# A fp32 network's third mixer with the value projection between two heads' scores, and its fourth mixer with the state space part in chunks of 8 steps

## The chip, the cores and the metric

The kernel runs on one core of one Trainium2 chip. The metric is the device time of one execution in microseconds (us); the number given for a kernel is the median of its runs. The engines have short names: PE (TensorE, matmuls), DVE (VectorE), ACT (ScalarE), POOL (GpSimd), SP (SyncE, which issues most of the DMAs).

## The reference, cut to what matters

The network has 512 positions and 1024 channels, in fp32. Two first layers (retention and stick breaking; gated recurrence) are followed by a second block: a third mixer, a SwiGLU feed-forward, a fourth mixer and another feed-forward, each inside `x + rmsnorm(fn(rmsnorm(x)))`. The change touches the third and the fourth mixer.

```
def even_mixer_2(t, ...):                       # third mixer
    proj = t @ w_in                             # q, k, v of 512 columns each, conv value and gate
    y_a = diff_attention(proj[..., :1536])      # 4 heads x 2 softmaxes of 64 dims, values of 128
    #   p = softmax(masked q k / 8);  w = p[:,:,0] - lam * p[:,:,1];  o = rmsnorm(w @ v, subln) * (1 - lam_init)
    y_b = conformer_conv(proj[..., 1536:])      # u = a * sigmoid(g); causal 31-tap depthwise conv; layernorm; silu
    return concatenate([y_a, y_b]) @ w_out

def odd_mixer_2(t, ...):                        # fourth mixer
    proj = t @ w_in                             # u of 256 columns, latents of 256 and 128, key rotation of 64
    y_c = s5_ssm(proj[..., :256])
    y_d = mla_attention(...)                    # 6 heads, 128 + 64 rotated dims, values of 128
    return concatenate([y_c, y_d]) @ w_out

def s5_ssm(u, ...):                             # 16 groups of 16 channels, 64 complex states each
    ab = exp(lr * dt) * (cos(li * dt) + i sin(li * dt))
    x[t] = ab * x[t-1] + bb @ u[t]              # complex, by associative_scan over 512 steps
    y = Re(c @ x) + d_skip * u
    z = gelu(y)
    return z * sigmoid(z @ w_glu + b_glu)
```

Both softmaxes are masked in chunks of 64 positions. The fp32 products of the projections are made of three passes each over operands split into a high and a low part.

## The kernel before, in words

The class `Net` writes one Python function per stage; a tile framework then sets the order of each engine's instructions once, by priorities (the order of the code, shifted by `self.prio(offset)`), by data and by free buffers. `hold(r, after)` adds a dependence by hand. An engine runs its instructions in that order.

Weights come in pieces of up to 512 KB: `wload` (L122) issues the DMA on SP into `wr` (3 buffers), ACT casts the high part `wh` (L133), DVE subtracts to get the low part `wl` (L116). `mm3` (L143) issues three matmuls (L145, L148, L149) for each product; `projT` (L155) gives outputs with channels on partitions, `projS` (L168) with positions on partitions. Activations lie in tiles `A4` (128 x 2048, 14 of them) and `U` (128 x 512, 13); PSUM has banks P (2), Z (3), W (2) and O (1). `outp` (L276) is an output projection with residual and norms; four of its weight pieces go into large buffers `wb`.

**Third mixer, `even2` (L722).** The convolution's gate is a sigmoid (L777). Three of its four channel blocks are made by 31 taps on DVE (L790), at a low rank; the fourth goes through `shifted` (L743, shifted copies by way of DRAM) and `conv_pe` (L758, matmuls L764). `scores(h)` (L815) computes a head's two softmaxes in four row blocks: matmuls L822, row maximum and exponential in `softmax_rows` (L413), difference L831, then transposes (`evac_wt`, tiles `pw` to `wt`). `av_` (L839) calls `head` (L372): value products L368, squares and a copy on ACT (L378, L379), a sum on DVE (L380). `stats` (L842), `norm` (L858) and `silu` (L863) finish the convolution's half, `heads` (L873) the attention's, in which `over_rms` scales by the root mean square. L884 to L897 set the sequence.

**Fourth mixer, `odd2` (L1017).** `s5_setup` (L924) runs during the feed-forward before it. It makes, for each of 8 pairs of groups (j), tables of cosine and sine over 512 steps and the input matrices, and stores them in DRAM (`rot`). In the mixer `s5(j, t)` (L1063) loads one table (`tab`), computes the input maps (`bur`, `bui`, L1070), rotates them (L1074 to L1076), makes two scans over 512 steps (L1077) and rotates back (L1078 to L1083); `s5_out` (L1088) multiplies by the output matrices into `py`. `s5_step` (L1101) places the eight: three ahead of the heads, one after each of the first five. `attn(hd)` (L1166) is a head's softmax, `av2` (L1182) its value product, issued in the next head. After the heads come gelu (L1208), the gated product and the sigmoid (L1220).

```
        for hd in range(6):
            attn(hd)
            s5_step(1, "P")
            if hd >= 2:
                self.lo(*late.pop(0))
```

## Time and profile before

| what | us |
|---|---|
| median of 3 runs | 1715.67 |
| lowest, highest run | 1712.09, 1715.69 |
| the profiled execution's own time | 1711.21 |
| its span, first to last instruction | 1709.4 |
| PE busy | 1656.5 |
| DVE busy | 950.2 |
| ACT busy | 677.7 |

The mean granted clock of TensorE is 0.987 of 2.4 GHz. A busy PE is not PE at its peak: matmuls are pipelined and their ends are modelled, so records overlap. "Idle before" names the engine or DMA that ended a wait. A window's line gives start and end from the span's start, its length, then busy us and instruction count of each engine, the granted clock and the DMA engines' share.

### The profile page before, as it was taken

Reading aid. Unit: us, or ns where it says so; the run is one execution under the profiler, and the core shown is the slowest. Engines: PE = TensorE matmul, PEld = TensorE weight load, DVE = VectorE, ACT = ScalarE, POOL = GpSimd, SP = SyncE. Lnnn points to the kernel's source line nnn. Section 1 sums busy time; section 2 is a strip of 40 time slices with the busy share of each in tenths; the row PEclk is TensorE's granted clock in tenths of the full one; section 3 lists DMA queues with packets and bytes.
Section 4 is the critical chain, followed back from the end, with each engine's and each line's share of the span. In section 5 each row is a group of like instructions: output and inputs, shape, how many; then the busy total and the mean of one; then the engine's idle time right before and its main releaser. Section 6 shows DMA issues by size and latency. Waiting matters only on the chain.

```text
span 1709.4 us, 20684 instructions
## 1 busy us (share of the span) xinstructions
PE 1656.5 (97%) x8072; PEld 1323.6 (77%) x8072; DVE 950.2 (56%) x1801; ACT 677.7 (40%) x1192; POOL 2.0 (0%) x8
## 2 busy tenths in 40 slices
PE   8999999999999999799999999999889999999998
PEld 8657788987789775588888878886447988888886
DVE  7564456765667994663222288468695622224332
ACT  6453334214545254643222254334556522223231
POOL 0000000000000000000000000000000000000000
PEclk9999999999999998899999999999999999999999
DMA  5212252202153220252222246432005332222341
GB/s 203 85 38 74 91 181 105 75 25 99 62 205 116 74 87 33 84 187 99 99 99 97 91 151 200 165 123 81 31 31 197 111 100 99 99 95 90 99 160 50
DMA packets 53169, 179.07 MB, mean 105 GB/s; under 512 B 5696, under 2 KB 8256, under 8 KB 52944
## 3 DMA queue, kind: packets, MB, share of 16 engines
q1 hardware_dynamic: 43824, 146.20, 25.6%
q10 hardware_dynamic: 9216, 31.48, 4.9%
q8 instruction: 63, 1.03, 0.2%
q14 instruction: 34, 0.28, 0.1%
q0 software_dynamic: 32, 0.07, 0.0%
HBM read 159.63 MB, written 18.10 MB: 104 GB/s over the span
## 4 chain that ended last, share of the span: by engine, by line
PE 85%; DVE 7%; ACT 4%; DMA 2%; issue 1%; ACTq 0%; DVEq 0%; SPq 0%
PE pp L145 17%; PE pp L148 17%; PE pp L149 17%; PE y L145 7%; PE y L149 7%; PE y L148 7%; PE pt L203 2%; PE po L368 2%; PE pl L625 1%; PE pw L203 1%; PE sc L822 1%; PE po L481 1%; DMA wr<-in_e2out 1%; PE pc L764 0%; DMA nw<-in_nw 0%
## 5 line engine op out<-in xcount | busy, mean ns | idle before, releaser
L116 DVE TENSOR_TENSOR wl<-wr,wh 128x1024 fp32r<-128x1024 f32 (+2 forms) x224 | 271.3, 1213 | 343.8 <-ACT wh L133 338.5
L133 ACT CAST wh<-wr 128x1024 fp32r<-128x1024 f32 (+2 forms) x224 | 233.4, 1043 | 523.4 <-PE pp L148 399.2
L148 PE MATMUL pp<-xl,wh 128*128 128x512 f32 (+1 forms) x1184 | 428.5, 362 | 0.0
L145 PE MATMUL pp<-xh,wh 128*128 128x512 f32 (+1 forms) x1184 | 426.0, 361 | 1.2 <-ACT xh L235 1.2
L149 PE MATMUL pp<-xh,wl 128*128 128x512 f32 (+1 forms) x1184 | 425.8, 360 | 0.0
L145 PEld LDWEIGHTS pp<-xh,wh 128*128 128x128 f32 x1184 | 223.8, 190 | 35.6 <-ACT xh L235 2.5
L148 PEld LDWEIGHTS pp<-xl,wh 128*128 128x128 f32 x1184 | 224.7, 190 | 33.8 <-issue 1.9
L149 PEld LDWEIGHTS pp<-xh,wl 128*128 128x128 f32 x1184 | 224.4, 190 | 33.4 <-issue 2.1
L145 PE MATMUL pp<-wh,xh 128*128 128x512 f32 (+1 forms) x320 | 126.4, 395 | 1.4 <-ACT sg L777 1.4
L148 PE MATMUL pp<-wl,xh 128*128 128x512 f32 (+1 forms) x320 | 126.5, 395 | 0.0
L149 PE MATMUL pp<-wh,xl 128*128 128x512 f32 (+1 forms) x320 | 125.4, 392 | 0.0
L145 PE MATMUL y<-wh,ah 128*128 128x512 f32 x288 | 112.7, 391 | 0.2
L148 PE MATMUL y<-wl,ah 128*128 128x512 f32 x288 | 112.3, 390 | 0.0
L149 PE MATMUL y<-wh,al 128*128 128x512 f32 x288 | 112.2, 389 | 0.0
L1238 DVE TENSOR_TENSOR act<-g,pp 128x512 f32<-128x512 f32 x44 | 30.2, 686 | 132.8 <-PE pp L149 131.4
L145 PEld LDWEIGHTS pp<-wh,xh 128*128 128x128 f32 x320 | 60.2, 188 | 13.4 <-ACT sg L777 1.8
L148 PEld LDWEIGHTS pp<-wl,xh 128*128 128x128 f32 x320 | 60.3, 188 | 11.7 <-issue 1.1
L149 PEld LDWEIGHTS pp<-wh,xl 128*128 128x128 f32 x320 | 60.2, 188 | 11.5 <-issue 0.6
L145 PEld LDWEIGHTS y<-wh,ah 128*128 128x128 f32 x288 | 54.1, 188 | 12.4 <-ACT bbz L998 1.1
L322 DVE TENSOR_TENSOR yn<-y,nw 128x512 f32<-128x512 f32 x48 | 31.8, 686 | 56.9 <-ACT yn L320 52.7
L790 DVE SCALAR_TENSOR_TENSOR ycv<-up,vec,ycv 128x512 f32<-128x512 f32 x90 | 63.2, 739 | 0.4
L149 PEld LDWEIGHTS y<-wh,al 128*128 128x128 f32 x288 | 54.1, 188 | 11.1
(381 smaller groups left out, 2335.0 us busy)
## 6 DMA issues: line engine op xcount, KB each, us to landing
wr<-in_f0gu SPq DMA_DIRECT2D x44, 512.0 KB, 3.3
wr<-in_f1gu SPq DMA_DIRECT2D x44, 512.0 KB, 3.3
wr<-in_f0d SPq DMA_DIRECT2D x22, 512.0 KB, 3.6
wr<-in_f1d SPq DMA_DIRECT2D x22, 512.0 KB, 3.4
xd<-x ACTq DMA_DIRECT2D x20, 512.0 KB, 2.7
x<-xd ACTq DMA_DIRECT2D x20, 512.0 KB, 6.1
wr<-in_o1t SPq DMA_DIRECT2D x16, 512.0 KB, 3.6
nw<-in_nw ACTq DMA_DIRECT2D x12, 512.0 KB, 7.8
```

What stands on the lines that cost most here:

```text
L116: return self.nc.vector.tensor_tensor(l, src, h.bitcast(F32), ALU.subtract)
L133: c = nc.scalar.copy(h, raw)
L145: r = mm(out, lhsT=a[0], rhs=b[0], start=first, stop=False)
L148: mm(out, lhsT=a[0], rhs=b[1], start=False, stop=False)
L149: return mm(out, lhsT=a[1], rhs=b[0], start=False, stop=last)
L203: self.nc.tensor.transpose(out, in_, self.ident)
L322: nc.vector.tensor_tensor(yn[j], yb[b][j], postw[j], ALU.mult)
L368: self.nc.tensor.matmul(po[:, tb * P : tb * P + P], lhsT=wt[:, sb, tb * P : tb * P + P], rhs=v[:, sb, c], start=sb == 0, stop=sb == tb)
L481: nc.tensor.matmul(po[r, sb * P :], lhsT=sv[:, sb, h * 64 : h * 64 + 64], rhs=wt[:, sb, sb * P :], start=sb == 0, stop=sb == 3)
L625: nc.tensor.matmul(pl[:, c4 * 64 : c4 * 64 + 64].rearrange("p (n x) -> p n x", x=H), lhsT=k[:, c4 * P : c4 * P + P], rhs=rh, start=True, s ...
L790: V.scalar_tensor_tensor(y, up[:, j : j + 512], self.v("dw", 4 * j + t), y, ALU.mult, ALU.add)
L1238: nc.vector.tensor_tensor(act[k // 4][:, k % 4], g, ps, ALU.mult)
```

## The change

**Third mixer.** The convolution's last two weight pieces are projected before the scores of head 1 instead of after. The value projection, which stood between the scores of heads 0 and 1, stands behind them at a rank lowered by 300 (its copies raised by 2000). `conv_pe(3)` stands before the scores of head 2 and is held until the last exponential of head 1. All four `av_` stand behind `silu`. The tap weights `dwd` are two tiles with a DMA each.

**Fourth mixer.** The state space part goes in 64 chunks of 8 steps. The set-up makes, besides powers of the state factor up to 8: an input matrix and an output matrix of each pair of groups for 8 steps x 16 channels (`s5m`), the kernel of the steps inside a chunk (`s5k`, read as a triangular matrix) and the rotation over 64 chunks (`s5r`). In the mixer u is written to DRAM and gathered so that the step within the chunk lies on partitions. `s5_in` does all groups at once: 32 matmuls with 64 columns, one rotation, two scans over 8 x 64, one rotation back. `s5_out(jj)`, in heads 0 and 1, makes half of the channels each: 24 matmuls with 64 or 63 columns, a copy, a scatter to DRAM in eight DMAs and a read back. Gelu is held until the last exponential of head 4, the sigmoid until that of head 5.

```diff
@@ -751,18 +751,21 @@
                 r = dr[32 * g : 32 * g + 32]
                 nc.sync.dma_start(u, bass.AP(tensor=r.tensor, offset=r.offset, ap=[[1, 4], [UW, 32], [1, 540]]))
                 us.append(u)
-            dwd = self.A4(name="dwd")[:, 0:2]
-            nc.sync.dma_start(dwd, self.A["dwd"])
-            cp[t] = us, dwd.rearrange("p a (m g c) -> p (a m) g c", g=4, c=32)
-        def conv_pe(t):
+            dwd = [self.U(name="dwd") for _ in range(2)]
+            for j in range(2):
+                nc.sync.dma_start(dwd[j], self.A["dwd"][:, j])
+            cp[t] = us, [d.rearrange("p (m g c) -> p m g c", g=4, c=32) for d in dwd]
+        def conv_pe(t, after):
...
+                    r = nc.tensor.matmul(pc[32 * g : 32 * g + 32], lhsT=dwd[m // 4][:, m % 4, g], rhs=us[g][:, 4 * m : 4 * m + 512],
+                                         start=m == 0, stop=m == 7)
+                    if m == 0:
+                        self.hold(r, after)
...
         scores(0)
-        self.projS("e2v", 512, lambda tb, ps: nc.scalar.copy(v[:, tb], ps))
+        self.projT("e2t", range(6, 8), conv)
         scores(1)
-        self.projT("e2t", range(6, 8), conv)
+        conv_pe(3, self.last_e)
+        def keep(tb, ps):
+            with self.prio(2000):
+                nc.scalar.copy(v[:, tb], ps)
+        with self.prio(-300):
+            self.projS("e2v", 512, keep)
         scores(2)
-        av_(0)
-        av_(1)
-        conv_pe(3)
         scores(3)
-        av_(2)
         stats()
-        av_(3)
         norm()
         silu()
+        for h in range(4):
+            av_(h)
...
+        def turns(c_dst, s_dst, steps, n):
+            bc = lambda f: f.unsqueeze(2).to_broadcast([P, 8, n])
+            sb = steps.unsqueeze(1).to_broadcast([P, 8, n])
+            m = self.U(8 * n, name="rm").rearrange("p (j n) -> p j n", j=8)
+            tt(c_dst, sb, bc(hi), ALU.mult)
+            V.tensor_scalar(m, c_dst, MAGIC, MAGIC, ALU.add, ALU.subtract)
+            tt(c_dst, c_dst, m, ALU.subtract)
+            tt(m, sb, bc(lo), ALU.mult)
+            b = self.U(8 * n, name="rb").rearrange("p (j n) -> p j n", j=8)
+            tt(b, m, c_dst, ALU.add)
+            sincos(c_dst, s_dst, b, m)
...
+        turns(pr, pi, dp, 16)
...
+        self.s5m = self.d_p.tile([P, 4 * 1024], F32, name="s5m")
+        self.s5r = self.d_p.tile([P, 3 * 512], F32, name="s5r")
+        self.s5k = self.d_p.tile([2 * P, 240], F32, name="s5k")
...
+                tt(m4, rh(bn[:, 0]), rp(p0, 0), ALU.mult)
+                tt(x4, rh(bn[:, 1]), rp(p1, 0), ALU.mult)
+                tt(m, m, x, op)
...
+                    self.tr(pt[:, P * c : P * c + P], m[:, P * c : P * c + P])
+                o = self.U(name="mt")
+                nc.scalar.copy(o, pt)
+                nc.sync.dma_start(self.s5m[:, 1024 * ri + 512 * jj : 1024 * ri + 512 * jj + 512], o)
...
+            pk = self.bank("W", "pk")
+            for c in range(4):
+                for (lo_, hi_, rhs) in ((0, 16, lambda ri: cn[:, ri, 4 * jj + c]),
+                                        (16, 128, lambda ri: go[ri][:, c, 0:7].rearrange("p t h -> p (t h)"))):
+                    for ri in range(2):
+                        nc.tensor.matmul(pk[32 * c : 32 * c + 32, lo_:hi_], lhsT=bb[:, ri, 4 * jj + c], rhs=rhs(ri),
+                                         start=ri == 0, stop=ri == 1)
+            kt = self.U(240, name="kt")
+            V.memset(kt[:, 0:112], 0.0)
+            nc.scalar.copy(kt[:, 112:240], pk[:, 0:P])
+            nc.sync.dma_start(self.s5k[P * jj : P * jj + P], kt)
...
+        turns(c64, s64, it, 64)
+        V.tensor_copy(r64, mag[:, :, 15:16].to_broadcast([P, 8, 64]))
+        V.memset(r64[:, :, 0:1], 0.0)
+        for i, f in enumerate((c64, s64, r64)):
+            nc.sync.dma_start(self.s5r[:, 512 * i : 512 * i + 512], f.rearrange("p j n -> p (j n)"))
...
+            nc.scalar.copy(uT[:, i].rearrange("p (s c) -> p c s", s=8), ps.rearrange("p (c s) -> p c s", s=8))
+            nc.sync.dma_start(ud[P * i : P * i + P], uT[:, i])
+            for s in range(8):
+                nc.sync.dma_start(ut[i][16 * s : 16 * s + 16].rearrange("p (g c) -> p g c", c=64), dv(ud)[:, s, 8 * i : 8 * i + 8])
...
+        def s5_in(after):
+            im, rt = self.A4(name="s5im"), self.A4(name="s5rt")
+            rot = [rt[:, i] for i in range(3)]
+            nc.sync.dma_start(im, self.s5m[:, 0:2048].rearrange("p (a d) -> p a d", a=4))
+            for i in range(3):
+                nc.sync.dma_start(rot[i], self.s5r[:, 512 * i : 512 * i + 512])
+            pz = [self.bank("Z", "z") for _ in range(2)]
+            imv = im.rearrange("p a d -> p (a d)").rearrange("p (r j m) -> p r j m", r=2, j=8)
+            first = True
+            for j in range(8):
+                for ri in range(2):
+                    for g in range(2):
+                        n = 2 * j + g
+                        r = nc.tensor.matmul(pz[ri][64 * g : 64 * g + 64, 64 * j : 64 * j + 64], lhsT=imv[:, ri, j, 64 * g : 64 * g + 64],
+                                             rhs=ut[n // 8][:, (n % 8) * 64 : (n % 8) * 64 + 64], start=True, stop=True)
+                        if first:
+                            self.hold(r, after)
+                            first = False
...
             for o, p0, p1, op in ((yr, pr, pi, ALU.add), (yi, pi, pr, ALU.subtract)):
                 V.tensor_tensor(a, p0, ct_, ALU.mult)
@@ -1077,43 +1176,51 @@
                 V.tensor_tensor_scan(o, rb, a, 0.0, ALU.mult, ALU.add)
             V.tensor_tensor(a, yr, ct_, ALU.mult)
             V.tensor_tensor(b, yi, st_, ALU.mult)
...
+            for g in range(2):
+                V.tensor_tensor(xz[g][0][64 * g : 64 * g + 64], a[64 * g : 64 * g + 64], b[64 * g : 64 * g + 64], ALU.subtract)
+            V.tensor_tensor(a, yr, st_, ALU.mult)
+            V.tensor_tensor(b, yi, ct_, ALU.mult)
+            for g in range(2):
+                V.tensor_tensor(xz[g][1][64 * g : 64 * g + 64], a[64 * g : 64 * g + 64], b[64 * g : 64 * g + 64], ALU.add)
+            return [[f.rearrange("p (j c) -> p j c", c=64) for f in x] for x in xz]
+        def s5_maps(jj):
...
+                nc.sync.dma_start(mt[:, ri], self.s5m[:, o : o + 512])
...
+            for s in range(8):
+                nc.sync.dma_start(tv[16 * s : 16 * s + 16], kv[:, 8 * jj : 8 * jj + 8, 112 - 16 * s : 240 - 16 * s])
...
+        def s5_out(jj, x, omv, tv):
+            py = self.bank("P", "py")
+            for n in range(8 * jj, 8 * jj + 8):
+                j, g = n // 2, n % 2
+                o = (n % 8) * 64
+                nc.tensor.matmul(py[:, o : o + 64], lhsT=tv[:, n % 8], rhs=ut[jj][:, o : o + 64], start=True, stop=False)
+                for ri in range(2):
+                    nc.tensor.matmul(py[:, o + 1 : o + 64], lhsT=omv[:, ri, j % 4], rhs=x[g][ri][:, j, 0:63], start=False, stop=ri == 1)
+            yo = self.U(name="yo")
+            nc.scalar.copy(yo, py)
+            for s in range(8):
+                nc.sync.dma_start(dv(yd)[:, s, 8 * jj : 8 * jj + 8], yo[16 * s : 16 * s + 16].rearrange("p (g c) -> p g c", c=64))
+            y = self.U(name="yt")
+            nc.sync.dma_start(y, yd[P * jj : P * jj + P])
+            V.scalar_tensor_tensor(y, uT[:, jj], self.v("dsk", jj), y, ALU.mult, ALU.add)
+            ys[jj] = y
...
-        s5_step(2, "Z")
...
+                if pc == 0:
+                    xs = s5_in(kept)
...
             attn(hd)
-            s5_step(1, "P")
+            if hd < 2:
+                s5_out(hd, xs, *maps[hd])
+                maps[1] = s5_maps(1) if hd == 0 else None
             if hd >= 2:
                 self.lo(*late.pop(0))
+            if hd == 4:
+                gelu_after = self.last_e
         flush()
-        s5_step(8, "P")
...
+            r = nc.scalar.activation(yg[:, k].rearrange("p (c s) -> p c s", s=8), ys[k].rearrange("p (s c) -> p c s", s=8), AF.Gelu_apprx_tanh)
+            self.hold(r, gelu_after)
...
-            nc.scalar.activation(g, ps, AF.Sigmoid, bias=self.v("bglu", m))
+            r = nc.scalar.activation(g, ps, AF.Sigmoid, bias=self.v("bglu", m))
+            self.hold(r, self.last_e)
```

How the order of the instructions moves, at the places that the prediction speaks of (line numbers with the change are those of the changed kernel):

PE in the third mixer, from the end of head 1's scores to the convolution (`pc`); `pw` are transposes, `po` value products, `sc` scores. Before:

```order
L203 MATMUL pw_5499<-cst,e_5487 128x128
L368 MATMUL po_5740<-v_5065,wt_5478 128x128
L822 MATMUL sc_5552<-kT_4704,qT_4703 128x512
L203 MATMUL pw_5522<-cst,e_5510 128x128 x2
L822 MATMUL sc_5553<-kT_4704,qT_4703 128x512
L368 MATMUL po_5740<-v_5065,wt_5478 128x128 x2
L822 MATMUL sc_5643<-kT_4704,qT_4703 128x128
L822 MATMUL sc_5644<-kT_4704,qT_4703 128x128
L203 MATMUL pw_5546<-cst,e_5534 128x128 x3
L368 MATMUL po_5740<-v_5065,wt_5478 128x128 x3
L203 MATMUL pw_5571<-cst,e_5559 128x128 x4
L764 MATMUL pc_5607<-cu_5468,dwd_5476 32x512
```

and with the change, where `pp` are the projections that moved:

```order
L149 MATMUL pp_5462<-wh_5394,xl_3978 128x512
L825 MATMUL sc_5517<-kT_4704,qT_4703 128x128
L145 MATMUL pp_5462<-wh_5394,xh_3976 128x512
L148 MATMUL pp_5462<-wl_5395,xh_3976 128x512
L203 MATMUL pw_5321<-cst,e_5309 128x128 x3
L149 MATMUL pp_5462<-wh_5394,xl_3978 128x512
L145 MATMUL pp_5462<-wh_5400,xh_3977 128x512
L148 MATMUL pp_5462<-wl_5401,xh_3977 128x512
L765 MATMUL pc_5352<-cu_5241,dwd_5249 32x512
```

The value products are gone from here; projections stand between the scores and transposes, and the convolution follows the scores of 128 columns that open head 2.

ACT in the fourth mixer, at the end of head 0 (`wt` is the copy of transposed weights, `mo` of the value product, `e` exponentials and their scaling). Before:

```order
L361 COPY wt_9706<-pw_9749 128x4x128
L361 COPY wt_9706<-pw_9766 128x128
L420 ACTIVATE e_9802,nm_9800<-sc_9796,nm_9800 128x256
L1190 COPY mo_9812<-po_9807 128x512
L1177 ACTIVATE e_9802<-e_9802,rr_9804 128x256
```

and with the change, where `yo` is the copy of the first half's state space output:

```order
L361 COPY wt_9726<-pw_9769 128x4x128
L361 COPY wt_9726<-pw_9786 128x128
L1211 COPY yo_9814<-py_9789 128x512
L420 ACTIVATE e_9845,nm_9843<-sc_9839,nm_9843 128x256
L1300 COPY mo_9855<-po_9850 128x512
L1287 ACTIVATE e_9845<-e_9845,rr_9847 128x256
```

The copy that waits for the output map stands ahead of the next head's exponential.

DVE in the fourth mixer, at the first query rotation (`t`, L433). Before:

```order
L1077 SCALAR_TENSOR_TENSOR yr_9451<-s5sm,sa_9453 128x512
L1075 TENSOR_TENSOR sb_9454<-bur_9447,tab_9445 128x512
L1074 TENSOR_TENSOR sa_9453<-bui_9448,tab_9445 128x512
L1076 TENSOR_TENSOR sa_9453<-sa_9453,sb_9454 128x512
L1077 SCALAR_TENSOR_TENSOR yi_9452<-s5sm,sa_9453 128x512
L433 TENSOR_TENSOR t_9588<-pp_9580,cst 128x384
L434 TENSOR_TENSOR t_9589<-pp_9580,cst 128x6x32
L435 TENSOR_TENSOR t_9589<-pp_9580,cst 128x6x32
L1078 TENSOR_TENSOR sa_9453<-yr_9451,tab_9445 128x512
L437 TENSOR_TENSOR r_9587<-t_9588,t_9589 128x384
```

and with the change:

```order
L1173 TENSOR_TENSOR sa_9535<-z_9494,s5rt_9489 128x512
L1174 TENSOR_TENSOR sb_9536<-z_9495,s5rt_9489 128x512
L1175 TENSOR_TENSOR sa_9535<-sa_9535,sb_9536 128x512
L1176 SCALAR_TENSOR_TENSOR yr_9533<-s5rt_9489,sa_9535 128x512
L1174 TENSOR_TENSOR sb_9536<-z_9494,s5rt_9489 128x512
L1173 TENSOR_TENSOR sa_9535<-z_9495,s5rt_9489 128x512
L1175 TENSOR_TENSOR sa_9535<-sa_9535,sb_9536 128x512
L1176 SCALAR_TENSOR_TENSOR yi_9534<-s5rt_9489,sa_9535 128x512
L433 TENSOR_TENSOR t_9597<-pp_9589,cst 128x384
L1177 TENSOR_TENSOR sa_9535<-yr_9533,s5rt_9489 128x512
L1178 TENSOR_TENSOR sb_9536<-yi_9534,s5rt_9489 128x512
```

Ahead of the first rotation stood parts of single steps; now the single pass stands there up to its second scan (`yi`), with `z` from its input maps.

## Rows read from the trace of the kernel before

**Rows 1.** The page's first part: TensorE, busy us, share of the span, instructions.

```profile
PE 1656.5 (97%) x8072; PEld 1323.6 (77%) x8072; DVE 950.2 (56%) x1801; ACT 677.7 (40%) x1192; POOL 2.0 (0%) x8
```

**Rows 2.** Windows of the third mixer: start:end, length, busy us by engine, clock, DMA.

```profile
690.00:700.00 10.00, 4.47 (x34) 3.79 (x34) 3.66 (x15) 8.75 (x24) 0.00 (x0) 1.00 0.00 0
700.00:710.00 10.00, 7.28 (x27) 5.83 (x28) 8.71 (x29) 5.69 (x9) 0.00 (x0) 0.50 0.00 1
```

**Rows 3.** Windows of the fourth mixer: one head's stretch, and the stretch that ends it.

```profile
1252.90:1266.80 13.90, 12.16 (x44) 6.08 (x42) 12.09 (x27) 7.13 (x19) 0.00 (x0) 1.00 0.15 48
...
1280.70:1298.00 17.30, 15.38 (x50) 9.06 (x49) 9.64 (x15) 13.55 (x23) 0.00 (x0) 0.82 0.26 85
```

**Rows 4.** The chain that ended last, fourth mixer: start us, us, what.

```profile
1143.99 0.86 PE bur L1070 x2
...
1184.76 0.86 PE py L1094 x2
...
1252.06 0.60 DVE yi L1082
...
1253.44 0.55 PE pw L203 x3
...
1286.00 1.28 ACT L1208
...
1290.88 1.23 DVE wb L116
```

**Rows 5.** VectorE by line, 1208 to 1286 us: forms, count, busy us, mean ns, idle before.

```profile
L1076 DVE TENSOR_TENSOR sa<-sa,sb 128x512 f32<-128x512 f32 x10 | 6.9, 688 | 0.2
L1077 DVE TENSOR_TENSOR_SCAN yi<-s5sm,sa 128x512 f32<-128x512 f32 x5 | 6.1, 1224 | 0.2
```

**Rows 6.** TensorE's timeline, third mixer: start us, us, line, operation, count, idle before.

```profile
652.89 4.73 PE L368 MATMUL po<-v,wt 128*128 128x128 f32 x40
...
673.13 8.48 PE L764 MATMUL pc<-cu,dwd 128*32 128x512 f32 x64
...
681.80 0.70 PE L822 MATMUL sc<-kT,qT 64*128 64x256 f32 x4
...
691.94 0.63 PE L203 MATMUL pw<-cst,e 128*128 128x128 f32 x4 [1.07 <-DVE e L831]
...
702.07 1.96 PE L203 MATMUL pt<-cst,yS 128*128 128x128 f32 x8 [6.29 <-DVE yS L861]
...
714.10 0.63 PE L145 MATMUL y<-wb,mh 128*128 128x512 f32 x2
714.57 0.39 PE L148 MATMUL y<-wb,mh 128*128 128x512 f32 x1
```

**Rows 7.** ScalarE's timeline, third mixer.

```profile
647.00 0.69 ACT L420 ACTIVATE e<-sc,nm 128x512 f32<-128x512 f32 x1
...
670.63 0.60 ACT L378 ACTIVATE sq<-po 128x512 f32<-128x512 f32 x1
...
703.86 1.45 ACT L870 ACTIVATE m<-pt,vec 128x512 f32<-128x512 f32 x2 [3.01 <-PE pt L203]
...
711.46 2.93 ACT L133 CAST wb<-wr 128x1024 fp32r<-128x1024 f32 x3
```

**Rows 8.** The chain again, second feed-forward: the set-up's transposing matmuls.

```profile
1000.87 0.64 PE pbb L994 x16
```

**Rows 9.** TensorE's timeline, fourth mixer.

```profile
1206.43 0.44 PE L203 MATMUL pw<-cst,e 128*128 128x128 f32 x2
...
1213.11 2.32 PE L1187 MATMUL po<-wt,va 128*128 128x512 f32 x8
```

**Rows 10.** VectorE's timeline, fourth mixer: the first query rotation.

```profile
1190.11 0.56 DVE L433 TENSOR_TENSOR t<-pp,cst 128x384 f32<-128x384 f32 x1 [0.96 <-PE pp L149]
```

**Rows 11.** DMA issues: tile and source, count, KB each, median us to landing.

```profile
tab<-rot SPq DMA_DIRECT2D x8, 640.0 KB, 4.5
```

**Rows 12.** The page's costliest groups: TensorE weight loads, busy us, mean ns, idle before.

```profile
L145 PEld LDWEIGHTS y<-wh,ah 128*128 128x128 f32 x288 | 54.1, 188 | 12.4 <-ACT bbz L998 1.1
```

More of the change, by code (lines that the diff above doesn't have):

```diff
@@ L974, in s5_setup @@
             tt(o, o, den, ALU.mult)
[L977 to L981 removed]
+        it = self.U(64, name="it")
+        nc.gpsimd.iota(it, [[1, 64]], base=0, channel_multiplier=0, allow_small_or_imprecise_dtypes=True)
+        dp = self.st(16, "dp")
@@ new lines, in s5_setup @@
+        v3 = lambda n, name: self.U(8 * n, name=name).rearrange("p (j n) -> p j n", j=8)
+        pr, pi, mag = v3(16, "pwr"), v3(16, "pwi"), v3(16, "mag")
+        turns(pr, pi, dp, 16)
+        V.memset(mag[:, :, 7:8], 1.0)
+        rho3 = rho.unsqueeze(2)
+        V.tensor_copy(mag[:, :, 8:9], rho3)
+        for d in range(2, 9):
+            tt(mag[:, :, 7 + d : 8 + d], mag[:, :, 6 + d : 7 + d], rho3, ALU.mult)
+        for d in range(1, 8):
+            V.tensor_copy(mag[:, :, 7 - d : 8 - d], mag[:, :, 7 + d : 8 + d])
@@ L982, in s5_setup @@
+        tt(pr, pr, mag, ALU.mult)
+        tt(pi, pi, mag, ALU.mult)
+        bc, cc = (self.U(name=n).rearrange("p (r j h) -> p r j h", r=2, j=8) for n in ("s5b", "s5c"))
         self.hold(nc.sync.dma_start(bc, self.A["s5bc"][:, 0:2]), self.start)
-        self.rot = self.d_p.tile([8, P, 2 * S + 2 * P], F32, name="rot")
+        self.hold(nc.sync.dma_start(cc, self.A["s5bc"][:, 2:4]), self.start)
+        V.tensor_scalar(cc[:, 1], cc[:, 1], -1.0, None, ALU.mult)
         b8 = lambda f: f.unsqueeze(2).to_broadcast([P, 8, 32])
-        w = [self.U(256, name="bb").rearrange("p (j h) -> p j h", j=8) for _ in range(3)]
+        bb = self.U(name="bb").rearrange("p (r j h) -> p r j h", r=2, j=8)
@@ L987, in s5_setup @@
+        w = self.U(256, name="bw").rearrange("p (j h) -> p j h", j=8)
         for ri in range(2):
-            V.tensor_tensor(w[0], bc[:, ri], b8(fre), ALU.mult)
-            V.tensor_tensor(w[1], bc[:, 1 - ri], b8(fim), ALU.mult)
-            V.tensor_tensor(w[2], w[0], w[1], ALU.subtract if ri == 0 else ALU.add)
-            for jj in range(2):
+            tt(bb[:, ri], bc[:, ri], b8(fre), ALU.mult)
+            tt(w, bc[:, 1 - ri], b8(fim), ALU.mult)
+            tt(bb[:, ri], bb[:, ri], w, ALU.subtract if ri == 0 else ALU.add)
@@ L992, in s5_setup @@
                 pt = self.bank("W", "pbb")
                 for c in range(4):
-                    self.nc.tensor.matmul(pt[32 * c : 32 * c + 32, 0:P], lhsT=w[2][:, 4 * jj + c], rhs=self.ident, start=True, stop=True)
-                bb = self.U(name="bbz").rearrange("p (c d) -> p c d", c=4)
-                V.memset(bb, 0.0)
-                for c in range(4):
-                    nc.scalar.copy(bb[32 * c : 32 * c + 32, c], pt[32 * c : 32 * c + 32, 0:P])
-                o = 2 * S + ri * P
-                nc.sync.dma_start(self.rot[4 * jj : 4 * jj + 4, :, o : o + P].rearrange("c p d -> p c d"), bb)
@@ new lines, in s5_setup @@
+                o = self.U(name="mt")
+                nc.scalar.copy(o, pt)
+                nc.sync.dma_start(self.s5m[:, 1024 * ri + 512 * jj : 1024 * ri + 512 * jj + 512], o)
+            go = []
+            for ri, (p0, p1, op) in enumerate(((pr, pi, ALU.add), (pi, pr, ALU.subtract))):
+                g = self.U(name="mg")
+                g4 = g.rearrange("p (j t h) -> p j t h", j=4, t=8)
+                if ri == 0:
+                    tt(g4, rh(cn[:, 0]), rp(pr, 8), ALU.mult)
+                    tt(x4, rh(cn[:, 1]), rp(pi, 8), ALU.mult)
+                    tt(g, g, x, ALU.add)
+                else:
+                    tt(g4, rh(cn[:, 1]), rp(pr, 8), ALU.mult)
+                    tt(x4, rh(cn[:, 0]), rp(pi, 8), ALU.mult)
+                    tt(g, g, x, ALU.subtract)
+                nc.sync.dma_start(self.s5m[:, 2048 + 1024 * ri + 512 * jj : 2048 + 1024 * ri + 512 * jj + 512], g)
+                go.append(g4)
@@ L1158, in odd2 @@
                     nc.scalar.copy(t[:, tb, :n], ps[:, :n])
+        maps = {0: s5_maps(0)}
         todo = []
```

94 lines of the change are left out of this document (36 added, 58 removed).

## The prediction

> **What bounds the kernel now.** I read the page's first part, then the windows of the two mixers, then the chain, then the engines' timelines. TensorE (PE) is busy 1656.5 of 1709.4 us [rows 1]: time can come only from the few stretches in which PE waits or runs at the half clock, and any PE work added elsewhere is paid in full.
>
> The windows show two such stretches. In the third mixer PE is busy 4.47 us of 690 to 700 and 7.28 of 700 to 710, there at a granted clock of 0.50, which is its 1.2 GHz level after that idling [rows 2]. In the fourth mixer a head takes 13.90 us, of which PE is busy 12.16, ScalarE (ACT) 7.13 and VectorE (DVE) 12.09 [rows 3]. The chain there runs through DVE's state space steps into the exponentials' scale and PE's transposes [rows 4]: DVE takes its instructions in order, so a head's row maximum and reciprocal stand behind some 10.5 us of state space work (12 operations of 0.68 to 0.69 and two scans, of 1.17 and 1.22; by those rows 8.2 + 2.4 [rows 5]). DVE sets the pace, PE only seems full.
>
> **The third mixer.** Before, PE leaves the projections at 652.9, does the two heads' value products (4.73 us), scores of head 2 with its waits, the convolution at 673.13 (8.48 us), and scores of head 3 from 681.80 to 692.6, 10.8 us with nothing in between [rows 6]. The exponentials of head 1 end at 647.7 [rows 7]. The change puts all four heads' value products behind the silu, the convolution behind that last exponential and the value projection, at a lower rank, into the gaps. The order of PE's instructions shows how far this goes: of the 144 moved projection matmuls (96 of the values, 48 of the convolution's last two pieces) 110 still stand ahead of the convolution and 34 behind it. I price them at nothing: they fill gaps in which PE waits for the softmax of heads 2 and 3, and 34 times 0.235 us (0.47 from one pair's start to the next matmul's, at 714 [rows 6]), 8.0, is less than those gaps: a head's scores are five times the 0.70 of the 256-column group [rows 6], with ten transposes of 0.12 it is 4.7 us of the 10.8. Head 1 still ends at about 647, because VectorE's convolution taps fill it there and their number does not change. Then: convolution 647.7 to 656, heads 2 and 3 at 10.8 us each, 678 against 692.6: 14.6 us earlier.
>
> Half of it is given back behind it. Before, silu began at 703.86 [rows 7] and the first output matmul with a large weight buffer ran at 714.10 [rows 6], 10.2 us later; three heads' squares and copies on ACT, 0.97 us a head (two operations like the one of 0.60 [rows 7], which overlap a little), lay in earlier gaps. Now all four stand behind silu's casts: casts end 4.9 us after silu begins, four heads 3.9, the last head's sum 0.69, the reciprocal root's 11 small operations about 1.0 (my estimate), four scalings at 0.69 [rows 5] 2.7, a transpose 0.5 (four passes of 0.118, below), its two copies 1.5 (as silu's pair of 1.45 [rows 7]), the weight's cast 1.05 (2.93 for three [rows 7]) and its low part 1.23 [rows 4]: 17.5, so 7.3 are lost. **Net: 7 us faster**; the ends are 14 (the heads' values are through while silu runs) and 0 (PE reaches the convolution no earlier).
>
> The split of the tap weights into two tiles and two DMAs costs nothing: they are issued well before the convolution, 512 KB in all as now.
>
> **The set-up of the state space part, in the second feed-forward's down projection.** PE is full there, so passes add up. Removed: two groups of 16 short passes, 0.64 us each [rows 8], 1.3. Added: 16 transposes and the 64 passes for the small kernel matrix. A 128-column fp32 pass takes 0.118 us (4.73 by 40 [rows 6]), a 32-column weight 0.04 (0.64 by 16 [rows 8]): 1.9 for the transposes, 2.6 to 7.5 for the 64, of which I take 4.5, as their weights have 32 columns but their streams up to 112. About 1 us for weights that come late, since VectorE's order has some 69 set-up operations in front of one weight's low half and SyncE a weight load behind a store. **6 us slower**; ends 3 and 13, the latter if that low half stalls PE for two weights.
>
> **The fourth mixer up to head 0.** Removed from PE before head 0: three pairs of input maps and six output maps 12 maps of 0.86 us for two passes [rows 4], some stretched to nearly 1: about 11 us, less 2 to 3 for the new pass's 64 short ones (0.04 each, as the row of 16 [rows 8]). But DVE's query rotation, now at 1190.11 [rows 10], sets when head 0 can start. In the order of DVE's instructions six multiply-adds and both scans of the new single pass stand in front of it: 6 x 0.69 + 2.39 = 6.5 us. Its input maps stand, in PE's order, where an output map of now ends the stretch of 1184 [rows 4]. 1184 + 6.5 = 1190.5, so the rotation starts as before, PE idles some 9 us for its buffers, and head 0's first transpose stays at about 1206.4, as does head 0's value product at 1213.11 [rows 9].
>
> **Heads 0 to 5.** Gone is DVE's 84 us of steps (8 x 10.5), most of it here. Head 0 ends about 9 us after 1207. Then come 48 passes of the first half's output map. They stream 64 columns and load 128-column weights; I price them like the value products, whose record is 0.118 [rows 6]: 5.6 us, to 1221.6.
>
> Then ACT is what lasts longest. The copy of the output (yo) stands ahead of head 1's exponentials, and it waits for the output map. After it: about 8 us of head 1's own ACT chain (7.13 busy in a head [rows 3], and its waits), and 2.4 us because the second half's maps are loaded behind eight stores of yo (a read of 640 KB in 4.5 [rows 11]). 10.4 us, to 1232. Then the second half's map 5.6, value product and next scores 3.9, heads 2 to 4 at 8.1 us each, 24.4. That 8.1: PE's 12.16 of a head less eight passes of 0.43 is 8.7, in which ends overlap; adding starts gives 7.6. Last, the end stage, 17.30 now with ACT busy 13.55 [rows 3]: I take 13.3, the ACT chain of head 5 with gelu and sigmoid moved into it, including one more table load of 1.28 [rows 4]. Total: 1207 + 9 + 5.6 + 10.4 + 5.6 + 3.9 + 24.4 + 13.3 = 1279.2 against 1298, **18.8 us faster**; ends 10 (the new waits cost nearly twice) and 35 (heads at 7.6, no idling before head 0).
>
> **Sum.** -7 - 18.8 + 6 is about -20 on a profiled execution of 1711.2, whose span is 1709.4. The median of the runs shown is 4.5 above that execution; with -20 I would see 1691 in a profiled execution and 1695 by the median of such runs; they spread from 1712.09 to 1715.69, so I take the middle, **1693**.
>
> **Rivals.**
> A, the forecast: 1693, its own range 1683 to 1703.
> B, more relief: the rotation is not held by the new pass, because its input maps run well before 1184 and DVE is free by then. The 9 us of idling go, and the yo copy finds its map done, 2.3 more: 1693 - 11 = 1682; with no tail lost in the third mixer 1675. For it: after the change DVE has no other state space work there. Against it: the input maps' hold on the last key copy.
> C, small passes cost a whole weight load. A weight load of 128 columns is recorded with 188 ns where PE is dense [rows 12]. If each of the 96 output passes took that, 96 x 0.070 = 6.7; 64 input passes likewise up to 7; 64 in the set-up 3: +17, 1710. Against it: 0.118 for 40 passes in a row [rows 6]. By the Trainium skill ("TensorE: Matmul & The Clock Gate", section "LDWEIGHTS (loading the stationary operand)") a load takes its columns divided by 1.2 in ns, whatever its rows, 107 ns for 128 and 53 for 64: by that rule the output passes would come, as an estimate, to 5.1 us a half and the sum to a microsecond less, and C would be out; the two rows of 0.118 and 0.04 a pass agree with it, the 188 does not.
> D, **slower**: the state space input arrives late. u is now written to DRAM and gathered by eight DMAs in runs of 256 bytes, for each half; the 18 DMAs stand on SyncE's queue among weight loads that wait for free buffers. The single pass cannot start before the last gather, and VectorE, in order, holds the query rotation behind it. Each microsecond that the maps run after 1184 delays every head: from about 20 us on, a last gather after 1204, the whole gain is gone; at 1212 the time is 1693 + 28 = 1721. For it: no row prices such short runs. Now the state space input is used at 1143.99 [rows 4], and a 640 KB read lands in 4.5 [rows 11], so the gather has 40 us for 256 KB each way a half; this speaks against it. By the Trainium skill ("DMA: Bandwidth & Descriptors", section "Specifications") transfers under 512 bytes are not at line rate. By that rule the gather would be slower than the row's reads, which is this rival's mechanism; no run here shows by how much.
> E, the third mixer's change doesn't do what it says: 110 of 144 fillers are used up before the convolution and the two heads then wait as now. Gain 0 there: 1703 (1715.7 - 18.8 + 6).
>
> **Chances.** A 0.53, B 0.20, E 0.09, C 0.08, D 0.10. 0.2%, 3.4 us, is about what a measurement tells from no change: faster means under 1712.2. A, B, E and half of C: 0.86; same, the other half of C: 0.04; slower, D: 0.10. The range leaves out D and the outermost of B and C: 1672 to 1710.
>
> **What would show it.** Right: in the third mixer the convolution starts near 648 and silu near 689, then ACT shows four square-and-copy pairs in a row before the first large-buffer output matmul. In the fourth, heads 2 to 4 take about 8 us with DVE half idle; PE idles before head 0; ACT waits for PE at the first yo. PE's 64 set-up passes are 4 to 5 us. Wrong: a head still over 11 us; query rotation later than 1195 on the old scale (D); output passes over 0.15 us (C); no difference between the silu times of both kernels (E).

## The result, and the profile after

The change made the kernel **slower**: 1729.55 us (median of 5 runs) against 1715.67 (5 runs), ratio 1.0079 [1.006, 1.0098], 13.9 us. The forecast was 1693, range 1672 to 1710. The profiled execution of after took 1733.11 us (span 1731.3); it is the longest of its five, so the traces differ by 21.9.

The page of after, its first part and the granted clock by slices:

```profile
PE 1658.3 (96%) x8216; PEld 1338.4 (77%) x8216; DVE 878.3 (51%) x1710; ACT 670.5 (39%) x1174; POOL 1.6 (0%) x8
...
PEclk8999999999999999899999999998798999999999
```

VectorE has lost 71.9 us of work and TensorE gained 1.8 against [rows 1]: DVE's relief came. But the clock now dips in the fourth mixer's slices. Where the span went (starts in us from the span's beginning; the last column is the change's own part, the stretch from the row above):

```
                                   before    after   stretch
e2q weights loaded                 522.64   525.30    +2.7  same code
f0d weights (third mixer, up proj) 964.88   968.86    +1.3
o2t weights (set-up over)         1068.03  1077.49    +5.5
first query rotation              1190.11  1206.09    +6.5
first transpose of head 0         1206.43  1224.43    +2.0
last o2out weights (heads over)   1292.13  1312.06    +1.9
f1d weights                       1547.21  1569.01    +1.9  mostly same code
```

Stretches of the same code differ by 2 to 3 us between two traces, so smaller terms are not read from them. The set-up's 5.5 stands all the same: from the f0d to the o2t weights the eight traces with the new set-up take 108.3 to 108.7 us, the three with the old one 103.2 to 103.6. What a trace hides by this, the timed runs below decide.

**Third mixer.** TensorE's timeline of after, answering [rows 6]:

```profile
652.91 2.76 PE L765 MATMUL pc<-cu,dwd 128*32 128x512 f32 x18
...
684.68 0.61 PE L203 MATMUL pw<-cst,e 128*128 128x128 f32 x4
...
695.07 1.97 PE L203 MATMUL pt<-cst,yS 128*128 128x128 f32 x8 [2.23 <-DVE yS L864]
...
710.72 0.44 PE L203 MATMUL pt<-cst,on 128*128 128x128 f32 x2 [2.38 <-DVE on L391]
...
715.33 0.78 PE L145 MATMUL y<-wb,mh 128*128 128x512 f32 x1
```

and ScalarE's, answering [rows 7]:

```profile
696.87 1.45 ACT L873 ACTIVATE m<-pt,vec 128x512 f32<-128x512 f32 x2 [3.40 <-PE pt L203]
...
701.60 0.61 ACT L378 ACTIVATE sq<-po 128x512 f32<-128x512 f32 x1
...
706.25 0.60 ACT L378 ACTIVATE sq<-po 128x512 f32<-128x512 f32 x1 [1.62 <-PE po L368]
...
713.03 1.26 ACT L884 ACTIVATE mh<-pt,lqt 128x512 fp32r<-128x512 f32 x2 [5.71 <-PE pt L203]
...
729.76 1.04 ACT L133 CAST wh<-wr 128x1024 fp32r<-128x1024 f32 x1 [4.87 <-DMA wr<-in_e2out]
...
732.88 0.60 ACT L320 ACTIVATE yn<-y 128x512 f32<-128x512 f32 x1 [2.08 <-PE y L149]
```

Before, the first normalized output (`yn`) came here:

```profile
728.20 0.60 ACT L320 ACTIVATE yn<-y 128x512 f32<-128x512 f32 x1 [2.08 <-PE y L149]
```

The convolution starts 20 us earlier and silu 7.0, yet the first output matmul with a large weight buffer comes at 715.33, before at 714.10: four square-and-copy pairs, the last head's root and scaling, and the transposes now stand in a row behind silu. Then ScalarE waits 4.87 us for the projection's last weight piece, where it waited 2.24 before; TensorE waits 1.64 for that cast, before 0.60.

**Fourth mixer.** SyncE's timeline, the DMA issues ahead of head 0:

```profile
1156.49 0.38 SPq L1104 DMA_DIRECT2D s5u<-uT  x1
1158.58 0.30 SPq L1106 DMA_DIRECT2D uT<-s5u  x1
1170.05 0.35 SPq L126 DMA_DIRECT2D wr<-in_o2kv  x1
...
1172.13 0.42 SPq L1106 DMA_DIRECT2D uT<-s5u  x1
...
1176.41 1.84 SPq L1106 DMA_DIRECT2D uT<-s5u  x4
1186.17 0.35 SPq L126 DMA_DIRECT2D wr<-in_o2out  x1
1186.62 0.38 SPq L1149 DMA_DIRECT2D s5im<-s5m  x1
...
1193.17 0.90 SPq L1106 DMA_DIRECT2D uT<-s5u  x2
```

The eight gathers of the second half of u are strewn over 34 us between weight loads that wait for buffers (from 1140 to 1200 the queue's waits at the weight loads, `SPq L126`, come to 14.1 us put down to `DVE t L435` and 12.4 to `DVE wl L116`). The last two are issued at 1193.17; PE's second input map waits for them until 1198.65, and DVE's rotation stands behind the pass:

```profile
1198.65 1.15 PE L1159 MATMUL z<-uT,s5im 128*64 128x64 f32 x32 [1.20 <-DMA uT<-s5u]
...
1249.50 1.65 PE L1282 MATMUL sc<-kn,qn 128*128 128x384 f32 x2 [5.73 <-ACT e L420]
```

```profile
1206.09 0.53 DVE L433 TENSOR_TENSOR t<-pp,cst 128x384 f32<-128x384 f32 x1
...
1247.28 0.75 DVE L1216 SCALAR_TENSOR_TENSOR yt<-uT,vec,yt 128x512 f32<-128x512 f32 x1 [5.96 <-DMA yt<-s5y]
...
1268.24 0.75 DVE L1216 SCALAR_TENSOR_TENSOR yt<-uT,vec,yt 128x512 f32<-128x512 f32 x1 [3.24 <-DMA yt<-s5y]
```

The last two DVE rows and PE's second row are a wait that no step of the forecast had. The skip term D*u (L1216) reads the output back from DRAM, and it stands in DVE's order ahead of the next head's row maximum. ScalarE shows the same chain, and in head 5 a second one:

```profile
1238.11 0.59 ACT L1211 COPY yo<-py 128x512 f32<-128x512 f32 x1 [8.06 <-PE py L1209]
...
1248.67 0.69 ACT L420 ACTIVATE e<-sc,nm 128x512 f32<-128x512 f32 x1 [6.70 <-DVE nm L418]
...
1299.85 1.28 ACT L1322 ACT_TABLE_LOAD   x1
...
1302.73 1.28 ACT L420 ACT_TABLE_LOAD   x1
...
1306.15 1.28 ACT L1322 ACT_TABLE_LOAD   x1
```

From yo's copy (over at 1238.70) to the read-back value in use (1247.28) are 8.6 us; the exponential behind it (1248.67) waits 6.70. In head 5 gelu, exponential and gelu alternate, with three table loads. Windows of after (columns as in [rows 3]):

```profile
1276.69:1285.88 9.19, 8.32 (x35) 5.06 (x34) 2.58 (x12) 6.53 (x19) 0.00 (x0) 1.00 0.00 0
...
1240.00:1260.00 20.00, 14.11 (x70) 10.78 (x71) 2.69 (x10) 5.71 (x16) 0.00 (x0) 0.66 0.17 39
```

A head without waits takes 9.19 us with DVE at 2.58, against 13.90 and 12.09 [rows 3]: this is the gain that was forecast. Around the two halves' output it is lost, with PE idle for 5.9 of 20 us and the granted clock at 0.66.

### The profile page after: what moved, and what is told of

The parts are those of the page before. It is cut to its first block, busy times and chain, and to the rows that moved or that the text cites. A ratio compares the mean times of both kernels' runs of the same rounds, so it can differ in the third digit from the quotient of the medians.

```text
span 1731.3 us, 20911 instructions
## 1 busy us (share of the span) xinstructions
PE 1658.3 (96%) x8216; PEld 1338.4 (77%) x8216; DVE 878.3 (51%) x1710; ACT 670.5 (39%) x1174; POOL 1.6 (0%) x8
## 4 chain that ended last, share of the span: by engine, by line
PE 84%; DVE 6%; ACT 4%; DMA 3%; issue 1%; SPq 0%; ACTq 0%; DVEq 0%
PE pp L145 17%; PE pp L148 17%; PE pp L149 17%; PE y L149 7%; PE y L145 7%; PE y L148 7%; PE pt L203 2%; PE po L368 1%; PE pl L625 1%; PE pw L203 1%; PE sc L825 1%; DVE wl L116 1%; DMA wr<-in_e2out 1%; PE po L1297 1%; PE sc L1282 1%
## 5 line engine op out<-in xcount | busy, mean ns | idle before, releaser
L116 DVE TENSOR_TENSOR wl<-wr,wh 128x1024 fp32r<-128x1024 f32 (+2 forms) x224 | 271.3, 1213 | 374.5 <-ACT wh L133 362.7
L145 PE MATMUL pp<-xh,wh 128*128 128x512 f32 (+1 forms) x1184 | 425.8, 361 | 1.2 <-ACT xh L235 1.2
L145 PEld LDWEIGHTS pp<-xh,wh 128*128 128x128 f32 x1184 | 223.9, 190 | 35.8 <-ACT xh L235 2.5
L145 PE MATMUL pp<-wh,xh 128*128 128x512 f32 (+1 forms) x320 | 127.1, 397 | 2.6 <-ACT sg L780 2.2
L145 PE MATMUL y<-wh,ah 128*128 128x512 f32 x288 | 112.6, 391 | 0.5 <-ACT mt L1054 0.5
L145 PEld LDWEIGHTS pp<-wh,xh 128*128 128x128 f32 x320 | 60.6, 189 | 15.8 <-ACT sg L780 2.9
L145 PEld LDWEIGHTS y<-wh,ah 128*128 128x128 f32 x288 | 54.1, 188 | 12.0 <-ACT mt L1054 0.6
L148 PEld LDWEIGHTS y<-wl,ah 128*128 128x128 f32 x288 | 54.1, 188 | 11.0 <-issue 0.2
```

Source lines behind the costliest of these rows:

```text
L116: return self.nc.vector.tensor_tensor(l, src, h.bitcast(F32), ALU.subtract)
L145: r = mm(out, lhsT=a[0], rhs=b[0], start=first, stop=False)
L148: mm(out, lhsT=a[0], rhs=b[1], start=False, stop=False)
```

## The experiments

My theory after these readings: the loss lies in the fourth mixer, in the gathers' places on SyncE's queue and in the skip term's place on DVE's. Its rival: the third mixer, whose tail gives back what it gained, carries it. Ratios are to the kernel before, on the same chip; where two experiments are compared, the us between them are the difference of their ratios.

**m3_alone**: the kernel before with the third mixer of the change.

```diff
-        self.projS("e2v", 512, lambda tb, ps: nc.scalar.copy(v[:, tb], ps))
...
+        conv_pe(3, self.last_e)
...
+        with self.prio(-300):
+            self.projS("e2v", 512, keep)
...
+        for h in range(4):
+            av_(h)
```

> The kernel before with the third mixer's change alone. Theory: the third mixer brings nothing by itself, because what the earlier convolution gains is lost behind the silu and in the output projection that follows it; the whole kernel is then within 3 us of the kernel before (1713 to 1719). Rival (the forecast's step): 7 us faster, about 1709. Second rival: the 2.7 us by which the changed kernel's trace is late ahead of the third mixer belongs to this part too; then 3 to 5 us slower.

1717.07 (7 runs), ratio 1.0021 [1.0006, 1.0037], +3.6 us. The third mixer's change brings nothing, and costs a little. Where, its trace does not show: from the e2q weights to the first normalized output it takes 205.6 us, and before 205.6.

**m4_alone**: the kernel of the change with the third mixer of before.

```diff
-        conv_pe(3, self.last_e)
...
+        av_(0)
+        av_(1)
+        conv_pe(3)
```

> The kernel before with the set-up and the fourth mixer's change alone. Theory: this part carries all of the loss, 5 us in the set-up and 8 to 11 in the mixer: 1728 to 1733. Rival: the two parts share it, because the third mixer's new order delays what follows; then this part alone is within 8 us of the kernel before.

1727.86 (6 runs), 1.0087 [1.0073, 1.01], +15 us: the fourth mixer, with its set-up, carries the loss. The next five runs are this kernel with one or more edits.

**m4_skip_late**: the skip term leaves s5_out and is held behind the last exponential of head 2, and of head 3 for the second half (counted from 0; the expectation counts from 1).

```diff
-            V.scalar_tensor_tensor(y, uT[:, jj], self.v("dsk", jj), y, ALU.mult, ALU.add)
...
+            r = V.scalar_tensor_tensor(ys[jj], uT[:, jj], self.v("dsk", jj), ys[jj], ALU.mult, ALU.add)
+            self.hold(r, self.last_e)
```

> Fourth mixer alone, with VectorE's operation on the state space output (uT, dsk, yt) held behind the last exponential of heads 3 and 4, so that it no longer stands in front of a row maximum while its data goes to DRAM and back. Theory: the two waits of 6.0 and 3.2 us of VectorE for yt in the changed kernel's trace go, and the half clock behind them; 8 to 13 us faster than the fourth mixer alone, about the time of the kernel before plus 4. Rival: the wait was hidden by the yo copy and the maps' loads and something else is late at the same place (the second half's maps); then under 3 us.

1725.03 (1715.89 to 1726.79, 4 runs), 1.0059 [1.0037, 1.0081]: 5 us better than m4_alone, just clear of noise (4.8, give or take 4.4) and short of the 8 to 13 expected. The trace kept is of its fastest run, 8 us below the next, so what it shows is worth more than the timed gain; the wait for the maps that the rival names is in it (below).

**m4_loads_early**: u's store and gathers, the input maps and the rotation table stand ahead of the weight loads on SyncE.

```diff
-            nc.sync.dma_start(ud[P * i : P * i + P], uT[:, i])
-            for s in range(8):
+            with self.prio(4000):
+              nc.sync.dma_start(ud[P * i : P * i + P], uT[:, i])
+              for s in range(8):
```

> Fourth mixer alone, with the gathers of u and the loads of s5im and s5rt raised in rank, so that on SyncE's queue they stand ahead of the output projection's weights. Theory: the input maps run some 6 us earlier, the query rotation with them, and head 0's first transpose too: 5 to 8 us faster than the fourth mixer alone. Rival: the rotation waits for the single pass's 6.5 us on VectorE in any case and the gathers themselves are slow (256-byte runs); then under 2 us.

1722.87 (4 runs), 1.0058 [1.0045, 1.0071]: 5 us better. SyncE's, TensorE's and VectorE's timelines of this kernel:

```profile
1154.73 3.64 SPq L1099 DMA_DIRECT2D uT<-s5u  x8
...
1168.83 0.38 SPq L1143 DMA_DIRECT2D s5im<-s5m  x1
```

```profile
1186.81 2.09 PE L1153 MATMUL z<-uT,s5im 128*64 128x64 f32 x64
```

```profile
1196.32 0.53 DVE L433 TENSOR_TENSOR t<-pp,cst 128x384 f32<-128x384 f32 x1
```

and TensorE's of m4_alone:

```profile
1197.48 1.15 PE L1151 MATMUL z<-uT,s5im 128*64 128x64 f32 x32 [1.25 <-DMA uT<-s5u]
```

All gathers are issued by 1158.4 and both input maps run in one piece at 1186.81, where m4_alone has its second at 1197.48; the rotation comes 8.6 us earlier (1196.32 against 1204.91). The place on the queue made the input late, not the gather itself.

**m4_both**: the two edits together.

> Fourth mixer alone, with both edits: loads raised in rank and VectorE's skip operation held back. Theory: the two losses lie one behind the other and add, 5 us each by the timed runs (7.5 and 11 us by the traces): 1715 to 1719, the kernel before plus 3 to 6, of which 5.5 is the set-up. Rival: with an earlier head 0 another wait (the second half's maps behind the stores of yo) takes back one of them; then above 1721.

1719.97 (1712.06 to 1723.24, 12 runs), 1.0026 [1.0009, 1.0043]: they add, 10 us together, though the median lies 1 us above the expected range. It is still not faster than before, and its runs spread over 11 us. TensorE's timeline shows a third wait:

```profile
1236.60 0.41 PE L1201 MATMUL py<-uT,s5mt 128*128 128x64 f32 x2 [2.77 <-DMA s5mt<-s5k]
...
1246.23 4.58 PE L1294 MATMUL po<-wt,va 128*128 128x512 f32 x8
```

and SyncE's, what the second half's map waits for:

```profile
1227.48 3.65 SPq L1207 DMA_DIRECT2D s5y<-yo  x8
1231.17 0.92 SPq L1190 DMA_DIRECT2D s5mt<-s5k  x2
1232.56 0.34 SPq L1209 DMA_DIRECT2D yt<-s5y  x1
1232.95 0.90 SPq L1190 DMA_DIRECT2D s5mt<-s5k  x2
```

The last four of its loads are issued behind the eight stores of yo. After this wait of 2.77 us PE runs the second half's map at the half clock:

```profile
1241.19:1245.19 4.00, 4.00 (x21) 4.00 (x20) 0.00 (x0) 0.00 (x0) 0.00 (x0) 0.50 0.00 0
```

The map takes 9.6 us (1236.60 to 1246.23) and the value product 4.58 instead of 2.32.

**m4_gelu_last**: m4_both, and gelu held behind the last exponential of head 5, which saves the alternation of tables (two of the three table loads there).

```diff
-            self.hold(r, gelu_after)
+            self.hold(r, self.last_e)
```

> As m4_both, with gelu held until the last exponential of head 5, as in the kernel before, instead of head 4. Theory: between the exponentials of head 5 stand two gelus with three table loads of 1.28 us, so ACT's chain there is about 4 us longer than it need be; 2 to 4 us faster than m4_both. Rival: gelu then comes behind everything, and the gated product and the last two mixer channels wait for it; no change or up to 3 us slower.

1714.97 (1703.97 to 1725.31, 12 runs), 1.0001 [0.9979, 1.0023]: 4 us better than m4_both, which is within the noise of the two (4.8), and an even wider spread, with a wait of 2.04 for the map in its trace.

**m4_maps_early**: m4_gelu_last, and the loads of the output maps ahead of the stores on SyncE.

```diff
+            with self.prio(4000):
+              for ri in range(2):
+                o = 2048 + 1024 * ri + 512 * jj
+                nc.sync.dma_start(mt[:, ri], self.s5m[:, o : o + 512])
+              for s in range(8):
```

> As m4_gelu_last, with all ten loads of the second half's maps raised in rank, so that they stand ahead of the stores of yo on SyncE's queue. Theory: PE's wait of 2.0 to 2.8 us for s5mt goes, and with it the fall of the granted clock to 0.50 behind it, in which the second half's output map takes 9.6 us instead of 5.4; 4 to 8 us faster than m4_gelu_last, 1707 to 1711. Rival: the clock falls there without that wait, because ACT's chain of head 1 leaves PE idle in any case; then within 2 us of m4_gelu_last, with the clock at 0.50 over the second half's map in the trace.

1705.77 (1704.03 to 1709.52, 6 runs), 0.9954 [0.9936, 0.9972]: 8 us **faster than before**, 8 better than m4_gelu_last, its six runs within 5.5 us. Its SyncE queue, the first of the output passes with what follows them on TensorE, and a window behind the maps:

```profile
1201.11 3.75 SPq L1191 DMA_DIRECT2D s5mt<-s5k  x8
1228.18 3.64 SPq L1208 DMA_DIRECT2D s5y<-yo  x8
```

```profile
1222.07 0.33 PE L1202 MATMUL py<-uT,s5mt 128*128 128x64 f32 x2
...
1232.73 0.44 PE L1280 MATMUL sc<-kn,qn 128*128 128x128 f32 x2
```

```profile
1247.00:1257.00 10.00, 8.87 (x37) 5.30 (x36) 3.34 (x14) 6.94 (x19) 0.00 (x0) 1.00 0.00 0
```

No wait for the map is left, and the clock stays at 1.00, over the passes too. The edit did more than take the wait away: with its loads early the second half's map moved on TensorE, from among head 1's scores and transposes to directly behind the first half's, and all 96 passes of both run in one row from 1222.07 to 1232.7. What the lost wait, the clock and the new place are worth each, this run does not tell apart. Where each edit acts, by the starts of the heads' value products (us between them; 0 to 2 holds both output maps, 4 to 5 gelu):

```
                 0 to 2   2 to 3   3 to 4   4 to 5
before            31.44    14.86    13.89    16.14
after             46.25     9.19     9.65    18.74
m4_loads_early    46.33     9.19     9.65    18.68
m4_skip_late      34.86     9.29     9.65    19.22
m4_both           41.29     9.30     9.64    17.60
m4_gelu_last      41.67     9.30     9.64    11.58
m4_maps_early     29.45     9.30     9.65    11.58
```

The first column of m4_skip_late and m4_both differs mainly by the clock behind the wait. TensorE's timeline of m4_skip_late has a wait for the same loads, and behind it the map in 5.4 us and the value product in 2.38:

```profile
1241.56 0.41 PE L1199 MATMUL py<-uT,s5mt 128*128 128x64 f32 x2 [1.75 <-DMA s5mt<-s5k]
...
1246.94 2.38 PE L1292 MATMUL po<-wt,va 128*128 128x512 f32 x8
```

**m3_av_early**: the third mixer alone again, with the first three heads' value products ahead of the convolution's statistics and the last ahead of their scaling.

```diff
         scores(3)
+        av_(0)
+        av_(1)
+        av_(2)
         stats()
+        av_(3)
         norm()
         silu()
-        for h in range(4):
-            av_(h)
         heads()
```

> Third mixer alone, with the value products of heads 0 to 2 ahead of the statistics and head 3's between them and the normalisation, as in the kernel before; convolution and projection stay moved. Theory: the squares and copies no longer stand behind silu's casts, the first output matmul with a large buffer comes 10 us after silu instead of 18.5, silu itself 3 to 4 us later: 3 to 6 us faster than the third mixer's change alone, 1711 to 1714. Rival: what silu loses is what the tail gains (ACT has the same work in either place): within 2 us of the third mixer alone.

1711.31 (12 runs), 0.9977 [0.9963, 0.999], -4 us, where m3_alone lost 3.6. ScalarE's timeline: the squares now lie ahead of silu.

```profile
689.98 0.63 ACT L378 ACTIVATE sq<-po 128x512 f32<-128x512 f32 x1
...
700.87 1.45 ACT L873 ACTIVATE m<-pt,vec 128x512 f32<-128x512 f32 x2 [2.98 <-PE pt L203]
...
706.55 1.36 ACT L884 ACTIVATE mh<-pt,lqt 128x512 fp32r<-128x512 f32 x2 [0.84 <-PE pt L203]
```

Silu is 4.0 us later than in after, but the first output matmul with a large buffer comes 4.9 earlier:

```profile
710.44 0.63 PE L145 MATMUL y<-wb,mh 128*128 128x512 f32 x2
```

**all_mended**: the kernel of the change with this third mixer (the diff above) and m4_maps_early's fourth (the four diffs before it together).

> Both mixers changed: the third with the value products ahead as in m3_av_early, the fourth as in m4_maps_early. Theory: the parts do not touch each other, so their ratios to the kernel before multiply: 3 to 5 us from the third mixer on top of m4_maps_early, 1703 to 1708, faster than the kernel before and than each part alone. Rival: an earlier start of the fourth mixer changes nothing in it, but the runs' spread hides the sum: not told apart from m3_av_early.

1705.28 (1699.35 to 1711.27, 7 runs), 0.9945 [0.9925, 0.9964]: 9 us faster than before, and some 23 than the change. That its third mixer adds to m4_maps_early (0.9954) isn't shown by these runs. Its page:

```profile
PE 1642.0 (97%) x8216; PEld 1330.9 (78%) x8216; DVE 877.2 (52%) x1710; ACT 667.3 (39%) x1172; POOL 1.6 (0%) x8
...
PEclk8999999999999999899999999999899999999999
```

Of the clock's dips in the fourth mixer (8798 in after) one 8 is left, and PE is busy 16.3 us less than in after for the same instructions.

## Why the prediction was wrong, point by point

- **DVE sets the pace of a head** held: without its steps a head takes 9.2 to 9.65 us. The 8.1 was too low: PE is busy for 8.32 of 9.19 and idle for the rest, and idling in a head was priced at nothing. That is 2.6 us over two heads.
- **"so the rotation starts as before"** failed. This is rival D's mechanism, which I gave 0.10: the input came late by its place on an in-order queue. I argued from a DMA's landing time that the gather had 40 us, and did not read where the gathers stand on SyncE; they are issued up to 1193.17. Counted from the o2t weights the rotation stands at 122.1 us before, at 128.6 in after and at 123.0 in m4_loads_early: with the loads moved the step holds. On the old scale after's is 1196.6, past the 1195 that was set as D's sign. Its price, by the traces 6.5 us up to the rotation, and 5 when mended, is far from the 28 of D, so D alone does not explain the result.
- **The heads, "18.8 us faster"**, from head 0's first transpose to the end: 87.6 us against 85.7, thus 1.9 slower. Three things were missing or too small. The skip term's wait was not in the sum, though its instruction is in the diff: the stretch of 0 to 2 grew to 46.25 where the sum had some 34 (1213.1 to about 1247), and the trace with that instruction alone moved, a fast run of its kernel, has 34.86; timed the move is worth 5. The maps behind the stores were priced at 2.4; against m4_maps_early (29.45) the stretch is 12 longer where the half clock stands behind the wait (m4_gelu_last, 41.67) and 5 where the full clock does (m4_skip_late, 34.86), the map's new place included; timed it is 8. The end stage was priced 4.0 shorter than before; 4 to 5 went from 16.14 to 18.74 instead, and to 11.58 once gelu stood behind the last exponential, a gain that the timed runs do not clearly show. With all three mended the stretch is 68.7, 17.0 less than before: the term's size was right for a kernel that has none of these waits. Of these 17.0 the set-up takes 5.1 in that trace and the stretch from it to head 0's first transpose, forecast as unchanged, 4.6; the 7.3 left agree with the 8 timed.
- **The set-up, 6 us slower**: right, 5.5 in the trace. Rival C (a whole weight load for each small pass) fell: the first half's 48 output passes run from 1232.60 to about 1237.9, 0.11 us each, and 32 input passes in 1.15. The rule of the Trainium skill ("TensorE: Matmul & The Clock Gate", section "LDWEIGHTS (loading the stationary operand)") had put C out, and the trace agrees with it for the output passes: by the rule a load of their 128 columns is, as an estimate, 0.107 us. For the 64 columns of the input passes the rule gives 0.053, and they took 0.036 each; the 0.04 of [rows 8], for 32 columns, which I called in agreement, stands against 0.027. There the measurement decides.
- **The third mixer, 7 us faster**: the timed part is 3.6 slower. Up to silu it gained 9.6 us from the e2q weights on, not 14.6 (convolution some 2.5 later than forecast, the two heads 2 longer: the 10.8 us of head 3 "with nothing in between" held 20 value passes of 3.3 us before, so there was less room for fillers than I took). The tail from silu to the first large-buffer matmul was priced at 17.5 and took 18.46 against 10.24 before. That it came so near is in part luck: the 1.0 for the root's 11 small operations stood on no row, and they took 2.3 (707.60 to 709.86), while the low part's 1.23 was not waited for, as the first matmul (L145) reads the high part. Then came what I had not priced: from that matmul to the first normalized output 17.55 instead of 14.10, with PE's granted clock at 0.66 from 710 to 720, where it was 0.99 before (the half clock stood in 700 to 710 then [rows 2]), and PE's wait for the late weights 1.0 longer. Rival E gave the right number (no gain) by the wrong mechanism: its convolution does start 20 us earlier. m3_av_early shows that the tail was the cause: take the values' squares out of it and the part is 4 us faster than before, half of what was forecast.

Timed, the two parts are +3.6 and +15, and together +13.9, which their intervals just allow.

## What to carry to other kernels

When a change relieves the engine that sets the pace, list for every new instruction that waits for a DMA what stands behind it in its engine's or queue's order, and read that from the order, not from the DMA's landing time. A read-back through DRAM belongs behind the work that does not need it, and loads that have nothing to wait for belong ahead of stores that do. Read the order again after each such move: raising the loads of m4_maps_early moved 48 matmuls as well. A gain that was forecast and is missing may still be there: here five moves of existing instructions turned 13.9 us lost into 9 gained.

## What was unexpected of the hardware

Behind a short wait of TensorE the clock fell in one execution and not in another. In m4_both it stood at 1.00 up to a wait of 2.77 us; behind it the granted clock was 0.50, its 1.2 GHz level, for the 12 us of windows shown in part above, and 48 passes took 9.6 us. In m4_skip_late the same passes ran at 1.00, in 5.4, behind a wait of 1.75 us, although the clock had been at 0.69 from 1236 to 1240, ahead of that wait. In m4_gelu_last it was at 0.57 from 1232 to 1236, again ahead of its wait of 2.04, and at 0.50 behind it. So a wait goes with the half clock in these traces, but that the wait alone lowers it is not shown.

The two kernels whose traces have the half clock behind the wait spread over 11 and 21 us from run to run, m4_maps_early over 5.5; but all_mended, whose trace has no such wait, spread over 12. Whether the clock explains the spread stays open too.
